# RWKV preparation in a decoder layer: which engine issues the stores of the planes and the bonus

## The chip, the cores and the metric

The kernel runs on one core of a Trainium2 chip. A core has five engines, each with a queue of instructions of its own that it works off strictly in order: TensorE (PE) multiplies matrices, VectorE (DVE) and ScalarE (ACT) work element by element, GpSimd (POOL) does a few side jobs, and SyncE (SP) does no arithmetic and only issues DMAs. A DMA can be issued from ACT's queue as well as from SP's. The engines wait for one another through semaphores, and an instruction that waits holds up everything behind it in its own queue, DMA issues included.

The metric is the device time of the whole program in microseconds (us), the median of three runs. One more run was recorded by the hardware profiler; rows of its trace are quoted below. All times in a trace are counted from the start of its span.

## What is computed

One layer of a decoder, in float32, on 1024 tokens of width 1024: a SwiGLU half-step, then three mixers side by side (RWKV-7, sliding-window attention, cross-attention into 256 memory tokens) with a gate for each, then a second SwiGLU half-step. The change lies in the RWKV mixer. Cut to what matters there:

```python
def rwkv7_mix(p, mu, w0, w_up, a0, a_up, g_up, k_k, k_a, r_k, gn_g, gn_b):
    p = p + (p_prev - p) * mu
    r, k, v, wd, ad, gd = _split(p, RWKV_SIZES)
    w_log = -jax.nn.softplus(-(w0 + jnp.tanh(wd) @ w_up)) - 0.5
    decay = jnp.exp(-jnp.exp(w_log))
    a = jax.nn.sigmoid(a0 + ad @ a_up)
    kk = (k * k_k).reshape(B, S, H, N)
    kk = kk / jnp.maximum(jnp.sqrt(jnp.sum(kk * kk, axis=-1, keepdims=True)), 1e-12)
    k = k * (1.0 + (a - 1.0) * k_a)
    y = rwkv7_recurrence(r, decay, k, v, -kk, kk * a)
    ...
    y = y + jnp.sum(r * k * r_k, axis=-1, keepdims=True) * v
```

Here `p` is the projection of the normed tokens by `w_in`. The kernel runs the recurrence in chunks of 64 tokens: a preparation makes, for every pair of heads, five arrays per token ("planes": two that hold b and k with their decays, called `bk`, then `at`, `r` and `v`) and the last line's term (the "bonus", `m`), and stores them in DRAM. A later stage inverts a small triangular matrix per chunk, and a chain over the 16 chunks reads the planes back.

## The kernel before

**Tiles and stages.** Everything is held with features on the 128 partitions and tokens along the free axis, in halves of 512 tokens. In order of time: memory keys, first SwiGLU, the RWKV preparation (`rwkv_prep`, about 740 to 920 us of the trace), eight blocks of attention projections and eight of gates on TensorE while VectorE inverts (`rwkv_invert`), the chain (`rwkv_chain`), attention with the rest of the gates, the output projection, and the second SwiGLU.

**Weights.** A float32 product is made of three matmuls (`mm3`, L330 to L332): high part by high part, high by low, low by high. Each piece of weights of 128x512 is loaded by SP into one of five buffers `w_raw` (L255), ScalarE rounds it into `w_hi` (L264), VectorE subtracts to get `w_lo` (L266). There are eight pairs of `w_hi` and `w_lo`, so a cast at L264 waits until TensorE has done with the pair from eight pieces ago, and a load at L255 waits until L266 has read its buffer.

**The preparation.** `rwkv_prep` runs over four pairs of heads, numbered 0 to 3. For each it calls `rwkv_block` for k, r and v. A block is 48 matmuls of 128x512 into two PSUM banks `pr`, and two copies by ScalarE (L820) from there into `raw`; four banks serve these blocks, so a block can start once the block two before it has been copied out. Small products stand between the blocks' matmuls: `lora` (L891, decays of the next pair), `ss` (L850, sums of squares of k), `ab` (L963, the small matrices that are inverted) and `rk` (L850, the sums in the bonus). From a copied k block come, in turn, `k` (DVE L822, L823), its square (ACT L927, shown as `n`), the parts `ss_hi` (ACT L410) and `n_lo` (DVE L411), and then the `ss` products. The decays give `sz` (ACT L893, DVE L895 and the running sum L896) and `ep` (ACT L901).

**Stores.** The small matrices `ab` go out by SP (L967), from a single buffer. The five planes (L973, 512 KB each, in pieces of 256 bytes) and the bonus (L974, 512 KB in pieces of 4 KB) go out by ScalarE in `bonus()`, once per pair: 24 stores.

**What sets the order.** The kernel is written in a tile framework: a scheduler decides, when the program is built, in which place each instruction stands in its engine's queue, from its own estimate of when inputs will be ready, from priorities, and from a few orders that the code fixes (`keep_in_program_order`). So the text of the code doesn't give the order in a queue, and moving one kind of instruction to another queue can shift others.

Of the kernel before, what the change touches and what calls it, by code (L numbers as in the profile page):

```python
# [53 lines left out]
C = 64  # L54
# [153 lines left out]
class Builder:  # L208
# [650 lines left out]
    def rwkv_prep(self, u, pool, pk_d, ab_d, bonus_d, att_d):  # L859
        nc = self.nc  # L860
        V, S = nc.vector, nc.scalar
        keep = self.tc.keep_in_program_order
        t4 = lambda n: pool.tile([P, T], F32, tag="t4", name=n)
        ch = lambda x: x.rearrange("p (c t) -> p c t", t=C)
        smask = pool.tile([P, T], mybir.dt.bfloat16, name="smask", bufs=1)
        nc.gpsimd.memset(smask, 1.0)
        nc.gpsimd.memset(ch(smask)[:, :, 0:1], 0.0)
        low = t4("low")
        self.rwkv_block(12, u, low)
        S.activation(low[0:64], low[0:64], ACT.Tanh)  # L870
        low_hi, low_lo = self.raw_part("rawl", "low_hi"), pool.tile([P, T], F32R, name="low_lo", bufs=1)
        self.split(low, low_hi, low_lo)
        gd = t4("gd")
        self.rwkv_block(13, u, gd)
        S.activation(self.sg, gd, ACT.Tanh, scale=0.5)
        V.tensor_scalar(self.sg, self.sg, 1.0, None, ALU.add)
        heads = [(slice(q * 64, q * 64 + 64), q) for q in (0, 1)]
        plane = lambda n: pool.tile([P, NC_, C], F32, tag="plane", name=n, bufs=8)
        t4r = lambda n: pool.tile([P, T], F32R, tag="t4", name=n)

        def decays(p):
            sz, a = t4("sz"), t4("a")
            w = self.lora[:, p * P : (p + 1) * P]
            w_hi, w_lo = (pool.tile([P, P], F32R, name="lora_" + t, bufs=1) for t in ("hi", "lo"))
            self.split(w, w_hi, w_lo)
            for h in (0, 1):
                cols = slice(h * TH, (h + 1) * TH)
                to = [(sz, slice(0, 64), self.half_w0, self.psum("lora")), (a, slice(64, 128), self.half_a0, self.psum("lora"))]
                for i, (w, x) in enumerate(((w_hi, low_hi), (w_hi, low_lo), (w_lo, low_hi))):
                    for _, rows, _, ps in to:  # L890
                        keep(nc.tensor.matmul(ps, w[rows], x[rows, cols], start=i == 0, stop=i == 2))  # L891
                for dst, _, bias, ps in to:
                    S.activation(dst[:, cols], ps, ACT.Tanh, scale=0.5, bias=bias[:, p : p + 1])  # L893

            V.tensor_scalar(sz, sz, 1.0, None, ALU.add)  # L895
            V.tensor_tensor_scan(sz, smask, sz, 0.0, ALU.mult, ALU.add)  # L896
            ep = t4("ep")

            tables = keep(S.preload_act_table_set("natural_log_exp_and_others"))
            with self.tc.issue_after(tables.ins):  # L900
                S.activation(ep, sz, ACT.Exp, scale=-0.5 * DECAY)  # L901
                S.activation(sz, sz, ACT.Exp, scale=0.5 * DECAY)
            S.copy(self.wc[:, :, p], ch(ep)[:, :, C - 1])
            return sz, a, ep

        later = {"k": {}, "r": {}}
        for p in range(NPAIR):
            if p == 0:
                v = plane("v")

                self.rwkv_block(8 + p, u, v)
                k = t4("k")
                self.rwkv_block(4 + p, u, k)
                made = [decays(p)]
            elif p == 1:
                k = t4("k")
                self.rwkv_block(4 + p, u, k, {**later["k"], 2: lambda: made.append(decays(p))})
            else:
                k = t4("k")
                self.rwkv_block(4 + p, u, k, later["k"])  # L920
            em, a, ep = made.pop()

            at = plane("at")
            V.scalar_tensor_tensor(at[:, :, 1:], ch(k)[:, :, 1:], self.neg_kk[:, p : p + 1], ch(ep)[:, :, : C - 1], ALU.mult, ALU.mult)
            S.activation(at[:, :, 0], ch(k)[:, :, 0], ACT.Copy, scale=self.neg_kk[:, p : p + 1])
            n2 = t4("n2")
            S.activation(n2, k, ACT.Square, scale=self.vec("rwkv_k_k", p))  # L927
            n2_parts = self.halves_split("ss", n2, t4r("n2_lo"))
            m = t4("m")
            S.activation(m, a, ACT.Identity, scale=self.half_ka[:, p : p + 1], bias=self.one_ka[:, p : p + 1])  # L930
            V.scalar_tensor_tensor(a, a, 1.0, em, ALU.add, ALU.mult)
            V.tensor_tensor(m, m, k, ALU.mult)
            bk = [plane("bk") for _ in heads]
            for rows, q in heads:
                V.tensor_tensor(bk[1 - q][rows], ch(m)[rows], ch(em)[rows], ALU.mult)

            def normed():
                for h, cols, ps in self.head_sums(*n2_parts):
                    V.tensor_scalar(n2[:, cols], ps, 1e-24, None, ALU.max)
                S.activation(n2, n2, ACT.Ln)  # L940
                S.activation(n2, n2, ACT.Exp, scale=-1.0, bias=self.ln_half)

            r = plane("r")
            self.rwkv_block(p, u, r, {**later["r"], 7: normed})
            V.scalar_tensor_tensor(ch(m), ch(m), self.vec("rwkv_r_k", p), r, ALU.mult, ALU.mult)
            V.tensor_tensor(r, r, ch(ep), ALU.mult)
            V.tensor_tensor(a, a, n2, ALU.mult)
            for rows, q in heads:
                V.scalar_tensor_tensor(bk[q][rows], ch(k)[rows], self.vec("rwkv_k_k", p)[rows], ch(a)[rows], ALU.mult, ALU.mult)
            m_parts = self.halves_split("rk", m, t4r("m_lo"))  # L950

            if p:
                v = plane("v")

            def gram(p=p, at=at, bk=bk):

                for half in (0, 1):
                    ps = self.psum("ab")
                    for c in range(8):

                        for rows, q in heads[::-1]:
                            cc = half * 8 + c
                            keep(nc.tensor.matmul(ps[rows, c * C : (c + 1) * C], bk[q][rows, cc], at[rows, cc], start=True, stop=True))  # L963
                    ab = pool.tile([P, 8, C], F32, tag="ab", name="ab", bufs=1)
                    V.tensor_tensor(ab, ps.rearrange("p (c t) -> p c t", t=C), self.gmask[:, 0:1, :].broadcast_to([P, 8, C]), ALU.mult)
                    for q in (0, 1):
                        nc.sync.dma_start(ab_d[half * 8 : (half + 1) * 8, p, q].rearrange("c s t -> s c t"), ab[q * 64 : q * 64 + 64])  # L967

            def bonus(p=p, parts=m_parts, m=m, planes=(*bk, at, r, v)):
                for h, cols, ps in self.head_sums(*parts):  # L970
                    V.tensor_tensor(ch(m[:, cols]), ch(ps), planes[4][:, h * 8 : (h + 1) * 8, :], ALU.mult)
                for i, x in enumerate(planes):
                    nc.scalar.dma_start(pk_d[:, :, p, i * C : (i + 1) * C].rearrange("c p t -> p c t"), x)  # L973
                nc.scalar.dma_start(bonus_d[p], m)  # L974

            if p == 0:

                later = {"k": {6: gram}, "r": {2: bonus}}
            else:
                within = {3: lambda: made.append(decays(p + 1))} if p + 1 < NPAIR else {}  # L980
                self.rwkv_block(8 + p, u, v, {**within, 7: gram})
                later = {"k": {5: bonus}, "r": {}}

        for i, f in enumerate(ATT_BLOCKS[:ATT_FIRST]):
            self.att_block(f, u, att_d, lambda: t4("att"), later["k"] if i == ATT_FIRST - 1 else {})
# [705 lines left out]
```

## Time and profile before

| | |
|---|---|
| median of three runs | 2321.53 us (2320.19 to 2323.29) |
| the profiled execution, its own time | 2316.22 us |
| its span, first to last instruction | 2314.5 us |
| mean granted TensorE clock | 0.994 |
| TensorE busy | 98% of the span |
| VectorE, ScalarE, GpSimd busy | 72%, 44%, 4% |
| DMA | 417.68 MB, 180 GB/s on average |

TensorE is busy nearly all the time. So what counts in a stage is the little time in which TensorE is idle, and the clock it is granted while it runs. A row of a timeline gives the start and the length of an instruction in us, the engine and the line, what it writes and reads, and in brackets how long its engine had been idle and what ended that. "ACTq" and "SPq" mark the issue of a DMA from that engine's queue.

### The profile page before, as it was taken

Reading aid. Unit: us, or ns where it says so; the run is one execution under the profiler, and the core shown is the slowest. Engines: PE = TensorE matmul, PEld = TensorE weight load, DVE = VectorE, ACT = ScalarE, POOL = GpSimd, SP = SyncE. Lnnn points to the kernel's source line nnn. Section 1 sums busy time; section 2 is a strip of 40 time slices with the busy share of each in tenths; the row PEclk is TensorE's granted clock in tenths of the full one; section 3 lists DMA queues with packets and bytes.
Section 4 is the critical chain, followed back from the end, with each engine's and each line's share of the span. In section 5 each row is a group of like instructions: output and inputs, shape, how many; then the busy total and the mean of one; then the engine's idle time right before and its main releaser. Section 6 shows DMA issues by size and latency. Waiting matters only on the chain. (4 is left out here: it accounts for less than half of the span.)

```text
span 2314.5 us, 33492 instructions
## 1 busy us (share of the span) xinstructions
PE 2263.2 (98%) x11914; PEld 1847.6 (80%) x11914; DVE 1656.0 (72%) x2683; ACT 1008.1 (44%) x1856; POOL 94.9 (4%) x134
## 2 busy tenths in 40 slices
PE   8999999999999999999999999999989999999997
PEld 6778888888888777888878877878868778888887
DVE  6998666665698786995645466575899886666576
ACT  6522333454566553223444454235762223345452
POOL 0000000000000000001300000340000000000000
PEclk9999999999999999999999999999999999999999
DMA  7477544586644447325445334554456774557663
GB/s 271 166 264 249 178 150 168 170 293 201 192 164 156 108 119 193 121 96 180 142 139 176 122 108 151 189 176 168 167 188 233 260 249 167 169 189 268 207 192 118
DMA packets 280776, 417.68 MB, mean 180 GB/s; under 512 B 82304, under 2 KB 104320, under 8 KB 280352
## 3 DMA queue, kind: packets, MB, share of 16 engines
q1 hardware_dynamic: 231552, 388.20, 50.6%
q10 hardware_dynamic: 49056, 27.34, 4.3%
q8 instruction: 94, 1.54, 0.3%
q14 instruction: 74, 0.61, 0.1%
HBM read 284.89 MB, written 129.50 MB: 179 GB/s over the span
## 5 line engine op out<-in xcount | busy, mean ns | idle before, releaser
L264 ACT CAST w_hi<-w_raw 128x512 fp32r<-128x512 f32 x594 | 365.5, 619 | 732.7 <-PE px L331 138.4
L266 DVE TENSOR_TENSOR w_lo<-w_raw,w_hi 128x512 fp32r<-128x512 f32 x594 | 413.6, 699 | 219.3 <-ACT w_hi L264 196.1
L331 PE MATMUL po<-u,w_hi 128*128 128x512 f32 (+1 forms) x476 | 181.0, 380 | 0.0
L330 PE MATMUL po<-u,w_hi 128*128 128x512 f32 (+1 forms) x476 | 181.0, 380 | 0.0
L332 PE MATMUL po<-u,w_lo 128*128 128x512 f32 (+1 forms) x476 | 181.0, 380 | 0.0
L330 PE MATMUL pgate<-u,w_hi 128*128 128x512 f32 x384 | 155.5, 405 | 0.0
L332 PE MATMUL pgate<-u,w_lo 128*128 128x512 f32 x384 | 151.3, 394 | 0.0
L330 PE MATMUL px<-f,w_hi 128*128 128x512 f32 x352 | 139.6, 397 | 11.4 <-DVE u L604 8.6
L331 PE MATMUL pgate<-u,w_hi 128*128 128x512 f32 x384 | 149.8, 390 | 0.0
L330 PE MATMUL px<-u,w_hi 128*128 128x512 f32 x352 | 137.5, 391 | 4.5 <-ACT w_hi L264 2.3
L331 PE MATMUL px<-f,w_hi 128*128 128x512 f32 x352 | 138.2, 393 | 0.3 <-DVE f L411 0.2
L332 PE MATMUL px<-f,w_lo 128*128 128x512 f32 x352 | 137.9, 392 | 0.0
L331 PE MATMUL px<-u,w_hi 128*128 128x512 f32 x352 | 137.0, 390 | 0.8 <-DVE u L411 0.8
L330 PE MATMUL pz<-u,w_hi 128*128 128x512 f32 x352 | 137.1, 390 | 0.2 <-DVE m L604 0.2
L331 PE MATMUL pz<-u,w_hi 128*128 128x512 f32 x352 | 137.2, 390 | 0.0
L332 PE MATMUL px<-u,w_lo 128*128 128x512 f32 x352 | 137.0, 389 | 0.0
L332 PE MATMUL pz<-u,w_lo 128*128 128x512 f32 x352 | 137.0, 389 | 0.0
L411 DVE TENSOR_TENSOR u<-hid,u 128x512 fp32r<-128x512 f32 x114 | 78.3, 689 | 45.2 <-ACT u L410 44.4
L331 PEld LDWEIGHTS po<-u,w_hi 128*128 128x128 f32 x476 | 89.5, 188 | 17.1
L330 PEld LDWEIGHTS po<-u,w_hi 128*128 128x128 f32 x476 | 89.5, 188 | 17.1
L332 PEld LDWEIGHTS po<-u,w_lo 128*128 128x128 f32 x476 | 89.5, 188 | 16.9
L410 ACT CAST u<-hid 128x512 fp32r<-128x512 f32 x114 | 70.7, 620 | 64.9 <-DMA hid<-form_d 56.5
(357 smaller groups left out, 5149.7 us busy)
## 6 DMA issues: line engine op xcount, KB each, us to landing
w_raw<-in_ffn_in SPq DMA_DIRECT2D x220, 256.0 KB
hid<-form_d SPq DMA_DIRECT2D x154, 256.0 KB
w_raw<-in_win SPq DMA_DIRECT2D x112, 256.0 KB
ws<-in_ffn_out SPq DMA_DIRECT2D x88, 256.0 KB
form_d<-g SPq DMA_DIRECT2D x88, 256.0 KB
ffn_sum_d<-ws SPq DMA_DIRECT2D x88, 256.0 KB
w_raw<-ffn_sum_d SPq DMA_DIRECT2D x88, 256.0 KB
form_d<-h SPq DMA_DIRECT2D x66, 256.0 KB
```

What stands on the lines that cost most here:

```text
L264: self.nc.scalar.copy(hi, x)
L266: self.nc.vector.tensor_tensor(lo, x, hi.bitcast(F32), ALU.subtract)
L330: mm(out, wh, xh, start=first, stop=False, **kw)
L331: mm(out, wh, xl, start=False, stop=False, **kw)
L332: mm(out, wl, xh, start=False, stop=last, **kw)
L410: self.nc.scalar.copy(hi, x)
L411: self.nc.vector.tensor_tensor(lo, x, hi.bitcast(F32), ALU.subtract)
```

## The change

The 24 stores of the planes and the bonus are issued from SP's queue instead of ScalarE's. Their sources, their destinations and their sizes stay as they are.

```diff
                 for i, x in enumerate(planes):
-                    nc.scalar.dma_start(pk_d[:, :, p, i * C : (i + 1) * C].rearrange("c p t -> p c t"), x)
-                nc.scalar.dma_start(bonus_d[p], m)
+                    nc.sync.dma_start(pk_d[:, :, p, i * C : (i + 1) * C].rearrange("c p t -> p c t"), x)
+                nc.sync.dma_start(bonus_d[p], m)
```

In the built program the scheduler then also places other instructions differently, in the preparation and in the inversion behind it. Three places matter in what follows.

The first is ScalarE's queue while pair 1 is finished and pair 2 begun (`raw<-pr` is here the copy of the k block of pair 2). Before:

```order
L899 ACT_TABLE_LOAD
L973 DMA pk_d<-bk 128x16x64
L901 ACTIVATE ep<-sz 128x1024
L973 DMA pk_d<-r 128x16x64
L264 COPY w_hi<-w_raw 128x512
L902 ACTIVATE sz<-sz 128x1024
L903 COPY wc<-ep 128x16
L973 DMA pk_d<-v 128x16x64
L974 DMA bonus_d<-m 128x1024
L820 COPY raw<-pr 128x512 x2
```

In the changed program, at the same place:

```order
L899 ACT_TABLE_LOAD
L901 ACTIVATE ep<-sz 128x1024
L264 COPY w_hi<-w_raw 128x512
L902 ACTIVATE sz<-sz 128x1024
L903 COPY wc<-ep 128x16
L820 COPY raw<-pr 128x512
L264 COPY w_hi<-w_raw 128x512
L820 COPY raw<-pr 128x512
```

The four stores are gone, and the cast at L264 ahead of L902 is now one that waits for a matmul in the middle of the k block itself; before, it waited for the second last matmul of the r block, which comes a whole block later. The two copies now stand around the cast that waits for the end of the k block.

The second place is VectorE's queue in pair 1, from the mask of the first `ab` of pair 0 to the low part of the square of k. Before:

```order
L895 TENSOR_SCALAR sz<-sz 128x1024
L965 TENSOR_TENSOR ab<-ab,gmask 128x512
L896 TENSOR_SCALAR sz<-smask,sz 128x1024
L971 TENSOR_TENSOR m<-rk,v 128x512 x2
L822 TENSOR_TENSOR k<-raw 128x1024
L266 TENSOR_TENSOR w_lo<-w_raw,w_hi 128x512
L965 TENSOR_TENSOR ab<-ab,gmask 128x512
L823 TENSOR_SCALAR k<-k,vecs,raw 128x1024
```

In the changed program:

```order
L965 TENSOR_TENSOR ab<-ab,gmask 128x512
L895 TENSOR_SCALAR sz<-sz 128x1024
L896 TENSOR_SCALAR sz<-smask,sz 128x1024
L822 TENSOR_TENSOR k<-raw 128x1024
L971 TENSOR_TENSOR m<-rk,v 128x512
L823 TENSOR_SCALAR k<-k,vecs,raw 128x1024
L266 TENSOR_TENSOR w_lo<-w_raw,w_hi 128x512
L965 TENSOR_TENSOR ab<-ab,gmask 128x512
L924 TENSOR_SCALAR at<-k,neg_kk,ep 128x16x63
L411 TENSOR_TENSOR n_lo<-n_7257,ss_hi 128x512 x2
```

What moved is small on VectorE; on TensorE the four `ss` products of each pair moved with it. Before, they stood 15, 48, 36 and 36 matmuls behind the end of the r block of pairs 0 to 3; now they stand directly behind it in all four.

The third place is SP's queue in pairs 0 and 1, with the loads of weights at L255. Before:

```order
L255 DMA w_raw<-in_win 128x512 x14
L967 DMA ab_d<-ab 64x8x64 x2
L255 DMA w_raw<-in_win 128x512
L967 DMA ab_d<-ab 64x8x64 x2
L255 DMA w_raw<-in_win 128x512 x5
```

In the changed program, a piece from pair 1:

```order
L255 DMA w_raw<-in_win 128x512
L973 DMA pk_d<-at 128x16x64
L255 DMA w_raw<-in_win 128x512
L973 DMA pk_d<-r 128x16x64
L973 DMA pk_d<-bk 128x16x64
L255 DMA w_raw<-in_win 128x512
L973 DMA pk_d<-bk 128x16x64
L967 DMA ab_d<-ab 64x8x64
```

The stores now stand between the loads of weights and the stores of `ab`.

## Prediction

> **What bounds the kernel now.** I read the page first, for the busy shares.
>
> ```profile
> span 2314.5 us, 33492 instructions
> PE 2263.2 (98%) x11914; PEld 1847.6 (80%) x11914; DVE 1656.0 (72%) x2683; ACT 1008.1 (44%) x1856; POOL 94.9 (4%) x134
> ```
>
> TensorE is the bound: a change gains only what TensorE stands still or runs at a lowered clock, and loses only what makes it stand still longer. The stores lie between 740 and 920 us, so next come windows there (busy time of each engine, granted clock PEclk, DMA share, GB/s).
>
> ```profile
> 740.00:920.00 180.00, 174.29 (x978) 138.36 (x977) 139.24 (x152) 89.47 (x134) 3.74 (x14) 0.99 0.53 132
> 830.80:834.20 3.40, 0.00 (x0) 0.00 (x0) 0.69 (x1) 2.10 (x5) 0.00 (x0) 1.00 1.04 200
> 835.70:839.10 3.40, 3.40 (x9) 2.65 (x8) 2.84 (x3) 1.36 (x2) 0.00 (x0) 0.50 0.30 121
> 875.70:878.00 2.30, 0.14 (x2) 0.07 (x1) 0.69 (x1) 1.32 (x4) 0.00 (x0) 1.00 0.73 143
> ```
>
> Of 180 us TensorE is busy 174.29, so 5.7 us are all that it is idle in the preparation, and nearly all of it lies in the second and the fourth stretch. The third runs at half the clock. The waits of 740 to 930 us (sum, count, longest) name what it waits for.
>
> ```profile
> PE pr L330 <- ACT raw L820: 5.6, 2, 3.4
> ACT w_hi L264 <- PE pr L331: 47.7, 20, 4.4
> ACT w_hi L264 <- DMA w_raw<-in_win: 2.1, 1, 2.1
> SPq L255 <- DVE w_lo L266: 142.7, 34, 10.4
> ```
>
> Twice, 5.6 us in all, the v block's first matmul waits for the copy of the k block (L820) out of the PSUM banks. ScalarE otherwise waits for TensorE, and for a load of weights only once. SP waits 142.7 us for buffers: its queue is mostly empty. The timeline shows the first stall (pair 2) and the second (pair 3).
>
> ```profile
> 827.68 0.39 PE L332 MATMUL pr<-u,w_lo 128*128 128x512 f32 x1
> 830.40 0.39 PE L332 MATMUL pr<-u,w_lo 128*128 128x512 f32 x1
> 830.60 0.62 ACT L264 CAST w_hi<-w_raw 128x512 fp32r<-128x512 f32 x1 [2.29 <-PE pr L331]
> 830.61 0.37 ACTq L973 DMA_DIRECT2D pk_d<-v  x1
> 831.07 2.47 ACTq L974 DMA_DIRECT2D bonus_d<-m  x1
> 831.13 1.05 ACT L902 ACTIVATE sz<-sz 128x1024 f32<-128x1024 f32 x1
> 833.59 1.07 ACT L820 COPY raw<-pr 128x512 f32<-128x512 f32 x2 [1.30 <-issue]
> 834.22 0.50 PE L330 MATMUL pr<-u,w_hi 128*128 128x512 f32 x1 [3.43 <-ACT raw L820]
> ...
> 875.58 0.62 ACT L264 CAST w_hi<-w_raw 128x512 fp32r<-128x512 f32 x1 [2.76 <-PE pr L331]
> 876.05 1.20 ACTq L974 DMA_DIRECT2D bonus_d<-m  x1
> 877.30 1.07 ACT L820 COPY raw<-pr 128x512 f32<-128x512 f32 x2 [0.97 <-issue]
> 877.94 0.50 PE L330 MATMUL pr<-u,w_hi 128*128 128x512 f32 x1 [2.16 <-ACT raw L820]
> ```
>
> At 830.40 the last matmul of the r block of pair 2 starts. The banks of the k block, finished a whole block earlier, are still not copied, because in ScalarE's queue the copy stands behind a cast that waits for the end of the r block (2.29 us idle until 830.60), then L902, and then the issue of the bonus store, 2.47 us, of which 1.30 keep ScalarE idle. Pair 3 shows the same with 0.97 us of issue. So each stall has two causes in one queue: the place of the copy, and the price of the issue ahead of it. From 827.68 to 830.40 lie twelve steps, which makes 0.227 us for one matmul at full clock.
>
> **The change part by part.** *The stalls.* In the changed order the copy of the k block in pairs 2 and 3 stands at the k block's own end, around the cast for that end, and no store is ahead of it. The v block then finds its banks free a block (48 × 0.227 = 10.9 us) early: −3.43 and −2.16 us. *The clock.* The stretch at half clock begins 1.5 us after the first stall ends. Nine matmuls take 3.40 us where fifteen fit (1.4 us lost), and 0.50 of 3.40 us is 1.7; I take 1.6. No such stretch follows the stall of 2.16 us, so a stall between 2.2 and 3.4 us is what brings it on here. With the stall gone: −1.6 us.
>
> The Trainium skill, "TensorE: Matmul & The Clock Gate", section "Part 1: The HAM clock gate", says that the clock drops to half after at least one idle window of about 3.4 us, and that the windows run free of the program. The two stalls of the trace agree with it, and by it 3.43 us only just trips the gate, so timed runs of the kernel before may have been without the stretch.
>
> *The new place of `ss`.* The four `ss` products of each pair now stand directly behind the r block. They were 15 to 48 matmuls later, so what makes `n_lo` has lost up to 10.9 us of cover. Its pieces, by form (count | busy us, mean ns | idle before):
>
> ```profile
> L896 DVE TENSOR_TENSOR_SCAN sz<-smask,sz 128x1024 f32<-128x1024 bf16 x4 | 9.1, 2286 | 0.1
> L901 ACT ACTIVATE ep<-sz 128x1024 f32<-128x1024 f32 x4 | 4.2, 1059 | 2.7 <-DVE sz L896 2.7
> L895 DVE TENSOR_SCALAR sz<-sz 128x1024 f32<-128x1024 f32 x4 | 2.8, 689 | 3.5 <-ACT sz L893 3.5
> L820 ACT COPY raw<-pr 128x512 f32<-128x512 f32 x20 | 10.6, 580 | 2.3 <-issue 2.3
> L822 DVE TENSOR_TENSOR k<-raw 128x1024 f32<-128x1024 f32 x4 | 4.9, 1221 | 4.4 <-ACT raw L820 4.4
> L971 DVE TENSOR_TENSOR m<-rk,v 128x512 f32<-128x512 f32 x8 | 5.1, 673 | 0.0
> L823 DVE SCALAR_TENSOR_TENSOR k<-k,vecs,raw 128x1024 f32<-128x1024 f32 x4 | 5.1, 1281 | 0.1
> L266 DVE TENSOR_TENSOR w_lo<-w_raw,w_hi 128x512 fp32r<-128x512 f32 x35 | 24.0, 688 | 33.2 <-ACT w_hi L264 32.6 <-PE ss L850 0.4
> L965 DVE TENSOR_TENSOR ab<-ab,gmask 128x512 f32<-128x512 f32 x8 | 5.5, 686 | 1.8 <-DMA ab_d<-ab 1.6 <-DMA w_raw<-in_win 0.2
> L924 DVE SCALAR_TENSOR_TENSOR at<-k,neg_kk,ep 128x1008 f32<-128x1008 f32 x4 | 5.1, 1269 | 1.4 <-ACT ep L901 1.2
> L893 ACT ACTIVATE a<-lora,half_a 128x512 f32<-128x512 f32 x8 | 5.5, 686 | 0.0
> L411 DVE TENSOR_TENSOR n_lo<-n,ss_hi 128x512 fp32r<-128x512 f32 x8 | 5.1, 685 | 1.4 <-ACT ss_hi L410 1.4
> 903.57 2.08 PE L963 MATMUL ab<-at,bk 64*64 64x64 f32 x64
> ```
>
> Pair 1 is the tight one, because there the second copy stands behind `ep`. From the end t of the k block: a cast (0.6, as at 830.60), two of L893 (1.37), L895 (0.69) and the scan L896 (2.29) make t + 5.0; `ep` 1.06 and the copy 0.58 make 6.6; on VectorE L822, L971, L823, L266, L965 and L924 (5.82) make 12.4, and both `n_lo` (1.37) 13.8. TensorE arrives after the r block (10.9), a batch of `ab` (2.08) and four `rk` (0.9): t + 13.9. Margin zero; hand-overs between the engines can make it 1.3 us late, as long as the two `n_lo`. In pair 0 the same products come within a few tenths of their inputs; in pairs 2 and 3 both copies stand at the block's end, which takes some 6 us off this chain. I take +0.5 us for all, of 0 to 1.5.
>
> *The stores on SP.* Their issue costs what it costs on ScalarE, 0.37 (830.61) to 2.47 us (831.07) each: 24 of them 9 to 59 us, against 142.7 us in which SP waits for buffers. They can also hold SP until their source is written; the nearest rows are the stores of `ab` on the same queue.
>
> ```profile
> SPq L967 <- DVE ab L965: 10.6, 6, 3.5
> q10 hardware_dynamic: 41856, 12.58, 31.6%
> q1 hardware_dynamic: 13286, 10.92, 20.9%
> ```
>
> That is 1.8 us for each wait, for 24 stores 42 us; even with the dearest issue, 101 of 142.7 us. Queue q10 holds what ScalarE issued, 12.58 MB (24 × 0.52) in 31.6% of 180 us = 56.9 us, that is 2.4 us a store over the 16 engines. Together with q1's 37.6 us the ring of SP would carry 94.5 of 180 us. With five buffers and 34 loads (the waits of L255 above) in 180 us, a load has four casts' time, some 21 us, less its own flight, before its cast wants it; the six stores of a pair in a row are 14 us. So nothing from the side of the loads: 0, where the other end is the third rival below.
>
> *Behind the preparation.* The same matmuls follow. The inversion reads `ab` once its last store has landed, so its end moves with the preparation's, and its result is early anyway:
>
> ```profile
> 1058.86 1.92 SPq L1021 DMA_DIRECT2D dinv<-inv_d  x2
> 1071.86 0.51 PE L1013 MATMUL z<-z,dinv 64*64 64x64 f32 x10
> ```
>
> The issue is 13 us before the first use, so a few us of delay there would cost nothing.
>
> **Sum:** −3.43 − 2.16 − 1.6 + 0.5 = −6.7 us. Against the profiled execution's own 2316.22 (span 2314.5 and 1.7 around it) that is 2309.5. The median of the three runs is 5.3 above that execution, by something that no trace shows, so I carry the difference over: 2321.53 − 6.7 = **2314.8 us**.
>
> **Rivals.** *Only the issue goes.* The copies might still come late (if the order at run time is set by another wait), and what is saved is the idle of the issue, 1.30 + 0.97 = 2.3 us: 2319.2; with the first stall then at 2.1 us and the half clock gone too, 2317.6. For it: the rows at 833.59 and 877.30 say "issue". Against it: the wait of 2.29 us ahead of the cast at 830.60 stands before the copy and has no part in the issue.
>
> The Trainium skill, "DMA: Bandwidth & Descriptors", section "Issuing engines are not separate DMA queues", speaks for this one: DMAs of all engines run over the same 16 DMA engines, and issuing from another engine saves only that sequencer's time to initiate, usually little. By it the change is worth the 2.3 us at most. Here the row at 831.07 shows 2.47 us for one issue, and an in-order queue behind it.
>
> *The `ss` products become the wait.* VectorE's second mask of `ab` (L965) may only write once the earlier store of `ab` has landed, and that store now stands on the same queue behind loads and planes. L965 above waited 1.6 us for it in all, with the planes on another queue; one plane of 2.4 us ahead, in pairs 1 to 3, makes three stalls of about 2.4 us: 7.2 lost for 7.2 gained, 2321.5. Two planes ahead make 4.8 us each, over the length that brought on the half clock: 3 × (4.8 + 1.6) − 7.2 = +12, 2333.5. Against it: six us of slack in pairs 2 and 3.
>
> *Loads held behind the stores (slower).* A store on SP whose source isn't written yet stops all loads behind it. The place is SP's queue between L255 and L973; it decides once a load is later than the 21 us less its flight. Then casts (L264) wait for DMA, and since the copies L820 stand behind casts, each pair could have a stall like the one at 834.22: 4 × (3.43 + 1.6) − 7.2 = +12.9, 2334.4. For it: single waits of SP for a buffer reach 10.4 us already, and the planes are made late in a pair. Against it: the sums above, 101 of 142.7 and 94.5 of 180.
>
> *The half clock isn't there in the timed runs.* Then 1.6 us less is gained: 2316.4, still faster.
>
> **How the numbers follow.** About 0.2% (4.6 us) is what a measurement of this kernel can tell from no change: faster is below 2316.9, slower above 2326.2. The forecast, with or without the half clock, gets 0.55 (0.53 faster, 0.02 same); only the issue 0.13 (same); the `ss` wait 0.15 (0.05 faster, as a small one; 0.07 same; 0.03 slower); loads held 0.12 (slower); something not seen 0.05 (0.01, 0.02, 0.02). Faster 0.59, same 0.24, slower 0.17. The likeliest case alone spans 2312 (nothing new waits and the timed runs lose more to the clock) to 2317. The range takes in the issue case and the `ss` wait: 2311 to 2324.
>
> **What would show it.** Right: in 740 to 920 us TensorE busy for all but a few tenths, the granted clock 1.00, no wait of L330 for L820; copies of k in pairs 2 and 3 within a us of the k block's end; at most 1.3 us of waiting of `ss` for L411 in pair 1; L264 waiting for TensorE and not for `w_raw`; SP's wait for L266 smaller but still tens of us; the inversion's load some 7 us earlier. Wrong: `ss` products waiting over 1.5 us, casts waiting for loads, a new stretch at 0.50, or a gain in the preparation that the chain gives back by waiting for `dinv`.

## The result, and the profile after

| | before | after |
|---|---|---|
| median | 2320.43 us (8 runs, 2317.05 to 2323.29) | 2313.24 us (8 runs, 2306.71 to 2317.63) |
| after to before | | 0.9973, 95% interval 0.9964 to 0.9983 |
| the profiled execution, its own time | 2316.22 us | 2312.79 us |

The change makes the kernel 7.2 us faster by the medians; 2314.8 us was predicted. The two profiled executions lie only 3.4 us apart. To see what the change itself does, one measures the stretch that holds all that it moves: from the first `lora` product (L891) to the first product of the chain (L1013), with the same matmuls in between. Their views by line (shortest, median and longest ns, first and last start) of the kernel before:

```profile
L891 PE MATMUL lora<-low_hi,lora_hi x16: 389/496/502, 749.7 to 850.8; 64*128 64x512 f32 x16
...
L1013 PE MATMUL y<-center,f x256: 217/218/267, 1067.5 to 1165.0; 64*64 64x64 f32 x128
```

And of the kernel after:

```profile
L891 PE MATMUL lora<-low_hi,lora_hi x16: 388/495/500, 750.8 to 839.5; 64*128 64x512 f32 x16
...
L1013 PE MATMUL y<-center,f x256: 218/218/267, 1062.1 to 1159.4; 64*64 64x64 f32 x128
```

With the starts to the hundredth, the stretch has 317.75 us before and 311.26 after: 6.49 us less. It is called "the stretch" below. The first rows show why whole times are a blunt measure here: the kernel after came 1.1 us later to its preparation. Windows of the first SwiGLU, which the change doesn't touch, show a part of it; the first is the kernel after, the second the kernel before:

```profile
151.30:154.60 3.30, 3.30 (x9) 2.57 (x10) 2.72 (x5) 0.00 (x0) 0.00 (x0) 0.51 0.61 181
```

```profile
151.30:154.60 3.30, 3.30 (x15) 2.56 (x15) 3.18 (x6) 0.23 (x1) 0.00 (x0) 1.00 0.78 274
```

This execution of the kernel after had a spell at half clock there (0.51), the one of before had none. The same kernel, run once more (e8 below), has none at this place: such spells come and go between executions of one kernel.

The window of the preparation in the kernel after:

```profile
740.00:920.00 180.00, 176.71 (x1007) 143.04 (x1006) 140.26 (x153) 90.59 (x138) 2.89 (x14) 1.00 0.58 146
```

TensorE is busy 176.71 us there instead of 174.29, at a granted clock of 1.00 instead of 0.99. No matmul waits for a copy. By form, the matmuls of 740 to 930 us of the kernel after that still wait (count | busy us, mean ns | idle before them):

```profile
L963 PE MATMUL ab<-at,bk 64*64 64x64 f32 x256 | 8.3, 219 | 2.3 <-ACT w_hi L264 1.6 <-ACT a L893 0.4 <-DVE bk L949 0.3
L891 PE MATMUL lora<-low_hi,lora_hi 64*128 64x512 f32 x16 | 4.2, 456 | 0.4 <-DVE n L939 0.3
...
L850 PE MATMUL ss<-n_lo,bones_r 128*128 128x512 f32 x8 | 3.3, 407 | 0.7 <-DVE n_lo L411 0.7
```

The idle of 5.6 us before L330 is gone; 3.4 us of idle before small products are new. The timeline of ScalarE shows the copies of the k block of pair 2, which answer to the row at 833.59 of before:

```profile
820.88 0.59 ACT L820 COPY raw<-pr 128x512 f32<-128x512 f32 x1 [0.56 <-PE pr L332]
821.36 0.62 ACT L264 CAST w_hi<-w_raw 128x512 fp32r<-128x512 f32 x1
821.88 0.59 ACT L820 COPY raw<-pr 128x512 f32<-128x512 f32 x1
```

They now wait for the block itself (0.56 us for its last matmul). The two largest new waits, in pairs 1 and 2, in the timeline of the kernel after:

```profile
792.13 1.29 DVE L411 TENSOR_TENSOR n_lo<-n,ss_hi 128x512 fp32r<-128x512 f32 x2
793.47 0.50 PE L850 MATMUL ss<-n_lo,bones_r 128*128 128x512 f32 x1 [0.66 <-DVE n_lo L411]
...
846.56 1.28 DVE L949 SCALAR_TENSOR_TENSOR bk<-k,vecs,a 64x1024 f32<-64x1024 f32 x1
847.35 0.61 ACT L264 CAST w_hi<-w_raw 128x512 fp32r<-128x512 f32 x1
847.99 0.41 PE L963 MATMUL ab<-at,bk 64*64 64x64 f32 x7 [1.55 <-ACT w_hi L264]
```

The last row names ScalarE's cast, since that ended last before the start, but the products read `bk`, and VectorE finishes `bk` at 846.56 + 1.28 = 847.84. Why VectorE is so late there is taken up below. SP's waits in 740 to 930 us, where the stores now are:

```profile
SPq L255 <- DVE w_lo L266: 93.0, 30, 7.1
SPq L973 <- DVE bk L949: 16.3, 6, 8.3
SPq L973 <- DVE at L924: 11.8, 3, 7.6
```

SP holds a store up to 8.3 us until its source is written, and still waits 93 us for buffers of weights.

### The profile page after: what moved, and what is told of

The parts are those of the page before. It is cut to its first block, busy times and chain, and to the rows that moved or that the text cites. A ratio compares the mean times of both kernels' runs of the same rounds, so it can differ in the third digit from the quotient of the medians.

```text
span 2311.1 us, 33503 instructions
## 1 busy us (share of the span) xinstructions
PE 2260.1 (98%) x11914; PEld 1846.5 (80%) x11914; DVE 1657.2 (72%) x2683; ACT 1007.7 (44%) x1856; POOL 94.6 (4%) x134
## 5 line engine op out<-in xcount | busy, mean ns | idle before, releaser
L264 ACT CAST w_hi<-w_raw 128x512 fp32r<-128x512 f32 x594 | 365.3, 619 | 693.3 <-PE px L331 147.0
L330 PE MATMUL po<-u,w_hi 128*128 128x512 f32 (+1 forms) x476 | 180.9, 380 | 0.0
L330 PE MATMUL pgate<-u,w_hi 128*128 128x512 f32 x384 | 155.4, 405 | 0.0
L330 PE MATMUL px<-f,w_hi 128*128 128x512 f32 x352 | 140.5, 400 | 13.4 <-DVE u L604 10.1
L330 PE MATMUL px<-u,w_hi 128*128 128x512 f32 x352 | 137.4, 390 | 3.4 <-ACT vm L1296 1.4
L330 PE MATMUL pz<-u,w_hi 128*128 128x512 f32 x352 | 137.0, 390 | 0.2 <-DVE m L604 0.2
L330 PEld LDWEIGHTS po<-u,w_hi 128*128 128x128 f32 x476 | 89.5, 188 | 16.9
```

The lines of the kernel that those rows point to most:

```text
L264: self.nc.scalar.copy(hi, x)
L330: mm(out, wh, xh, start=first, stop=False, **kw)
```

## The experiments

All ratios are to the kernel before, run again on the same chip in the same set; medians of different sets can't be compared (that of the kernel before lies between 2319.97 and 2322.24 us in them). The stretch comes from each kernel's one trace.

| kernel | median, us | ratio, 95% interval | stretch, us | against before |
|---|---|---|---|---|
| before | 2320.43 | | 317.75 | |
| the change | 2313.24 | 0.9964 to 0.9983 | 311.26 | −6.49 |
| e1, only the bonus on SP | 2320.17 | 0.9981 to 1.0000 | 317.91 | +0.17 |
| e2, only the planes on SP | 2316.88 | 0.9964 to 0.9988 | 312.22 | −5.53 |
| e3, stores as before, copies first | 2323.15 | 0.9989 to 1.0008 | 317.01 | −0.74 |
| e4, the change, `ab` later | 2313.69 | 0.9945 to 0.9975 | 310.19 | −7.55 |
| e5, stores as before, copies and `ss_hi` first | 2308.59 | 0.9935 to 0.9962 | 308.89 | −8.85 |
| e6, the change, every store twice | 2334.60 | 1.0055 to 1.0081 | 335.77 | +18.02 |
| e7, the change, fewer waits | 2308.05 | 0.9936 to 0.9961 | 308.30 | −9.45 |
| e8, the change again | 2310.06 | 0.9944 to 0.9970 | 310.99 | −6.76 |
| e9, the change, `lora` split | 2312.17 | 0.9953 to 0.9977 | 310.54 | −7.21 |
| e10, as e7, `ab` later still | 2310.18 | 0.9939 to 0.9966 | 308.33 | −9.41 |
| e11, as e10, the last `ab` later too | 2310.87 | 0.9938 to 0.9963 | 307.87 | −9.87 |
| e12, as e11, stores on ScalarE | 2309.07 | 0.9933 to 0.9957 | 307.66 | −10.09 |

e8 is the yardstick: 

> The changed kernel itself once more, as a yardstick: the preparation 6.5 us shorter than before within 0.5 us, with the same four new waits of ss, ab and lora; the whole program differs from the first profile by up to 3 us through stretches at half clock in other stages.

It gave −6.76: this one repeat of the changed kernel lies within 0.3 us. The kernel before was traced only once.

### e1 and e2: one kind of store alone

e1 moves only the last line's store, e2 only the planes':

```diff
-                nc.scalar.dma_start(bonus_d[p], m)
+                nc.sync.dma_start(bonus_d[p], m)
```

> Only the four bonus stores move to SP; the twenty plane stores stay on ScalarE, and the order on TensorE stays that of before. Theory (the place of the copy in ScalarE's queue is the larger cause): the k copies still stand behind the cast for the r block's end, so L330 waits for L820 about 3.43 - 1.30 = 2.1 us and 2.16 - 0.97 = 1.2 us, 3.3 us in all instead of 5.6; the half clock behind the first stall is gone (1.6 us); the preparation gains 2.3 to 3.9 us. Rival (the price of the issue is the cause): both stalls vanish and it gains as much as the whole change, 6 to 7 us.

> Only the twenty plane stores move to SP; the four bonus stores, whose issues of 2.47 and 1.20 us stood ahead of the late copies, stay on ScalarE. The order on TensorE is that of the changed kernel. Theory (order): no wait of L330 for L820, the same new waits of the ab and ss products (about 3 us in all), gain in the preparation 6 to 7 us as with the whole change. Rival (issue): the issues of the bonus still hold the copies, L330 waits for them about 2 us in pairs 2 and 3 and the gain falls to 2 to 4 us.

TensorE's timeline of e1, at the two old stalls and one new one:

```profile
805.49 0.47 PE L850 MATMUL ss<-n_lo,bones_r 128*128 128x512 f32 x1 [2.50 <-DVE n_lo L411]
...
837.98 0.50 PE L330 MATMUL pr<-u,w_hi 128*128 128x512 f32 x1 [2.03 <-ACT raw L820]
...
879.03 0.50 PE L330 MATMUL pr<-u,w_hi 128*128 128x512 f32 x1 [1.08 <-ACT raw L820]
```

The stalls fell from 3.43 to 2.03 and from 2.16 to 1.08 us: by 1.40 and 1.08, which is what the issue rows of before promised (1.30 and 0.97). The rest of each stall stays, as the theory had it. But the expected gain was not kept: `ss` of pair 1 waits 2.50 us. ScalarE's timeline of e1 shows why:

```profile
798.23 1.14 ACT L927 ACTIVATE n<-k,vecs 128x1024 f32<-128x1024 f32 x1
...
802.79 0.62 ACT L264 CAST w_hi<-w_raw 128x512 fp32r<-128x512 f32 x1 [3.43 <-PE pr L331]
803.32 1.14 ACT L410 CAST ss_hi<-n 128x512 fp32r<-128x512 f32 x2
```

`n` is ready at 799.4, but the scheduler now put a cast that waits for the end of the v block of pair 1 ahead of `ss_hi`. In the kernel before, `ss_hi` stood ahead of that cast. So the same trap opened at another place, by the shift of one store. A stretch at half clock followed this stall (the last section shows it). In e2 no wait of L330 for a copy is left although the issues of the bonus stay on ScalarE, and the stretch is 5.53 us shorter: 1.0 to 1.2 us short of the whole change. Some 0.7 us of that are longer waits in pair 2 (`ab` 1.91 us instead of 1.55, and 0.35 of `ss`), and there VectorE had waited 3.81 us instead of 2.67 for a store of `ab` to land. What is left isn't shown to be a cost of the four issues.

### e3 and e5: no store moved

e3 gives only the copies a higher priority:

```diff
-                nc.scalar.copy(raw[:, 8 + h * TH : 8 + (h + 1) * TH], ps[h])
+                with self.tc.high_priority(offset=30):
+                    nc.scalar.copy(raw[:, 8 + h * TH : 8 + (h + 1) * TH], ps[h])
```

> All 24 stores stay on ScalarE; only the copies at L820 get a higher priority, which puts the copies of the k block at that block's end in pairs 2 and 3. Theory (order): the two stalls and the half clock go without any store moved: 5.6 + 1.6 = 7.2 us less in the preparation, with the lora products still in three groups per pair, and the ss products late as before, so without the new waits of ss; up to 1 us may come back elsewhere. Rival (issue): the stores' issues delay ScalarE wherever the copies stand, and TensorE waits 2 us or more for copies, casts or ss_hi; gain under 4 us.

The stalls at L330 went, and the gain failed to come. TensorE's timeline of e3 (its lines are one higher than before's):

```profile
849.17 0.50 PE L851 MATMUL ss<-n_lo,bones_r 128*128 128x512 f32 x1 [2.41 <-DVE n_lo L411]
...
891.52 0.47 PE L851 MATMUL ss<-n_lo,bones_r 128*128 128x512 f32 x1 [2.50 <-DVE n_lo L411]
```

and the rows of ScalarE in front of the first of them:

```profile
846.57 0.62 ACT L264 CAST w_hi<-w_raw 128x512 fp32r<-128x512 f32 x1 [2.41 <-PE pr L331]
846.81 0.37 ACTq L974 DMA_DIRECT2D pk_d<-at  x1
847.09 1.14 ACT L410 CAST ss_hi<-n 128x512 fp32r<-128x512 f32 x2
```

Neither theory had this: the copies came out of the trap and `ss_hi` fell into it, in pairs 2 and 3. `ss_hi` follows the cast at once, with no idle time for the issue that stands between them, which speaks against the stores' issue as the cause. The stall lasts as long as the work behind the released cast: 2.60 us from its start to `ss` here, 2.69 in pair 3 (from 888.83), 2.70 in e1 (from 802.79). That the cast itself waited 2.41 us, like TensorE, is a coincidence; in e1 it waited 3.43 for a stall of 2.50. Half clock followed the stall of 2.50 in pair 3 and took its part of the gain too. e5 tests the order: it adds the same priority for the square of k and its parts.

```diff
-            S.activation(n2, k, ACT.Square, scale=self.vec("rwkv_k_k", p))
-            n2_parts = self.halves_split("ss", n2, t4r("n2_lo"))
+            with self.tc.high_priority(offset=30):
+                S.activation(n2, k, ACT.Square, scale=self.vec("rwkv_k_k", p))
+                n2_parts = self.halves_split("ss", n2, t4r("n2_lo"))
```

> All 24 stores stay on ScalarE, as before; the copies (L820) and the square of k with its parts (Square, ss_hi, n_lo) get a higher priority, so that in ScalarE's queue neither stands behind a cast that waits for a later matmul. On TensorE the lora products stand in six groups instead of ten. Theory (order alone): no wait of L330 for the copies and none of ss for n_lo; the preparation loses 7.5 us of stalls and half clock, and some 0.4 us for each of the four lora groups that are gone, 1.6 us: 8 to 9.5 us less than before, more than the change itself with its 6.5. Rival (the stores' issue on ScalarE costs by itself, wherever the other instructions stand): TensorE waits 2 us or more for ScalarE's late products and the gain stays under 6 us.

All 24 stores are still on ScalarE, and the stretch is 8.85 us shorter, more than the change brings. By form, in e5:

```profile
L330 PE MATMUL pr<-u,w_hi 128*128 128x512 f32 x179 | 70.3, 393 | 0.0
...
L851 PE MATMUL ss<-n_lo,bones_r 128*128 128x512 f32 x8 | 3.3, 407 | 0.0
```

Neither waits any more. The order alone does it, without a store moved. Some 2 us of the 8.85 are fewer breaks at the `lora` products (see e9): steps of 0.31 to 0.35 us went from 41 to 29, and three of the four of about 0.43 us are gone. The rest are stalls and the half clock.

### e4, e7, e10 and e11: the change's own waits

e4 emits `ab` of pairs 1 and 2 a little later:

```diff
-                self.rwkv_block(8 + p, u, v, {**within, 7: gram})
-                later = {"k": {5: bonus}, "r": {}}
+                self.rwkv_block(8 + p, u, v, {**within, 7: gram} if p + 1 == NPAIR else within)
+                later = {"k": {5: bonus} if p + 1 == NPAIR else {0: gram, 5: bonus}, "r": {}}
```

> The changed kernel with the ab products of pairs 1 and 2 emitted at the start of the next k block instead of at the end of the v block; on TensorE this puts pair 2's ab four matmuls (0.9 us) later. Theory (the changed kernel's own new wait, 1.55 us of ab for VectorE's bk in pair 2, comes from ab standing too early): that wait falls by 0.9 us to 0.7 us, the rest stays: 0.9 us less than the changed kernel. Rival (what makes bk is itself late by the wait of VectorE, so that whatever comes next waits): no gain, the wait only moves to another product.

In TensorE's timeline of e4 the wait of 1.55 us has become

```profile
848.24 0.47 PE L963 MATMUL ab<-at,bk 64*64 64x64 f32 x9 [0.57 <-ACT w_hi L264]
```

0.98 us less for four matmuls (0.9 us), and nothing waits in its place: −7.55 against −6.49. e7 goes on with that. It adds e3's priority for the copies, and the `ab` of pair 0 and the decays of pair 1 come later:

```diff
-                self.rwkv_block(4 + p, u, k, {**later["k"], 2: lambda: made.append(decays(p))})
+                self.rwkv_block(4 + p, u, k, {**later["k"], 4: lambda: made.append(decays(p))})
...
-                later = {"k": {6: gram}, "r": {2: bonus}}
+                later = {"k": {}, "r": {0: gram, 2: bonus}}
...
-                later = {"k": {5: bonus} if p + 1 == NPAIR else {0: gram, 5: bonus}, "r": {}}
+                later = {"k": {5: bonus} if p + 1 == NPAIR else {2: gram, 5: bonus}, "r": {}}
```

> The changed kernel (stores on SP) with the copies at a higher priority, ab of pair 0 two and of pairs 1 and 2 four to sixteen matmuls later, and the decays of pair 1 two pieces later. It aims at the changed kernel's own waits: lora for n 0.8, ab 0.5 + 1.7 + 0.5, ss 0.8, together 4.3 us. Theory (all of them are products placed ahead of what VectorE can deliver): 3 to 4 us less than the changed kernel in the preparation, that is 9.5 to 10.5 us less than before. Rival (VectorE is the bound there, the waits move to what comes next): less than 1 us gained on the changed kernel.

−9.45, just short of the 9.5 to 10.5 that were expected; 1.00 us of idle before `ab` of pair 0 and some 0.4 in pair 3 stay. e10 and e11 push those away too (`{1: gram, 3: bonus}` in pair 0 and `{3: gram, 6: bonus}` in pairs 1 and 2; e11 also `{0: gram, 5: bonus}` in pair 3):

> The kernel e7_fewer_waits with ab of pairs 0, 1 and 2 six more matmuls later. Theory (ab stands ahead of what VectorE delivers): of its two waits left, 1.17 us (pair 0) falls to 0 and 0.56 us (pair 3, not moved) stays; preparation 10.5 us less than before. Rival (VectorE is behind by then and the wait goes to rk, which comes next): no less than 9.5.

> As e10, with ab of pair 3 twenty-three matmuls (5 us) later too; the small matrices go out some 5 us later and the inversion begins that much later. Theory (the inverse is early by 12 us or more, as the prediction had it): preparation 11 us less than before, and the chain gives nothing back. Rival (the chain waits for dinv): a new wait of the chain, up to 5 us given back.

e10 missed: −9.41 instead of −10.5. The wait of pair 0 went, but 0.49 us came back as a wait of `ss` for `n_lo` in pair 1 (not at `rk`, where the rival had it), and three more long steps at changes of shape (25 instead of 22; see e9) came with the new order. e11 brought 0.46 us more, about the wait of pair 3 that it removes, and its chain gives nothing back though the last `ab` starts 4.2 us later (887.65 instead of 883.48).

### e12: the same with the stores on ScalarE

e12 is e11 with the 24 stores back on ScalarE's queue and the square of k at e5's priority.

> As e11, with all 24 stores on ScalarE as before and the square of k at a higher priority, so that the order is free of the late copies and late ss_hi; lora in four groups. Theory (the queue of the stores matters only through the order): preparation within 1.5 us of e11. Rival (24 issues on ScalarE cost by themselves): waits of TensorE for ScalarE's products of 3 us or more that e11 doesn't have.

307.66 against 307.87 us of stretch, and medians whose intervals overlap: once the order is good, the queue of the stores makes no difference that can be measured. The two orders aren't the same one: the priority of the square also shifts small products in e12. No run has the changed kernel's own order with all stores on ScalarE.

### e6: twice the stores

The changed kernel, in which all six stores of `bonus()` are issued a second time from SP.

> The changed kernel with every plane and bonus stored twice from SP, 48 stores instead of 24; pair 2's ab stands ten matmuls later than in the changed kernel. Theory (SP and its DMA ring have room): the casts at L264 don't wait for loads; the preparation is within 1 us of the changed kernel's, or up to 1.7 us shorter where pair 2's ab no longer waits. Rival (loads are held behind stores, and the changed kernel is close to that edge): casts wait for w_raw, TensorE loses 3 us or more in the preparation.

The time came out as the rival had it, 0.7% slower, but at another place than it named. The casts don't wait for loads. TensorE's one long wait in e6, with the copy it waits for:

```profile
946.90 1.07 ACT L1344 COPY att<-pq 128x512 f32<-128x512 f32 x2 [14.95 <-DMA att_d<-att]
947.54 0.80 PE L330 MATMUL pq<-u,w_hi 128*128 128x512 f32 x1 [16.01 <-ACT att L1344]
```

It is the attention copies behind the preparation that need a buffer whose store, also on SP, is stuck behind the planes of the last pair. A spell at half clock begins within the stall and lasts 3.4 us beyond it, and the chain waits 3.0 us for the load of the planes (`f`), which adds to the loss. So SP and its ring do have an edge, between 24 and 48 stores, and it is met where several stores of one pair come in a row.

### e9: the grouping of `lora`

The twelve `lora` products of pairs 2 and 3 are issued in three groups of four, at pieces 3, 4 and 5 of the v block:

```diff
-                within = {3: lambda: made.append(decays(p + 1))} if p + 1 < NPAIR else {}
+                d = decays(p + 1) if p + 1 < NPAIR else None
+                within = {3: lambda: next(d), 4: lambda: next(d), 5: lambda: made.append(next(d))} if d else {}
```

with `decays` made a generator that pauses after each of its three kinds of product.

> The changed kernel with the twelve lora products of pairs 2 and 3 issued in three groups of four, with six matmuls of the v block between them, instead of in one group: four groups more in the preparation. Theory (each change between the 64-row lora products and the 128-row matmuls costs TensorE about 0.1 us at four places, 0.4 us for a group): 1.7 us more at such changes than in the changed kernel, about eight to sixteen more steps of 0.31 to 0.35 us instead of 0.227. Rival (the grouping costs nothing, the difference between before and after had another source): as many such steps as in the changed kernel, 23, and no loss outside the waits that the trace names.

TensorE's timeline of e9 around one such group:

```profile
839.17 0.39 PE L331 MATMUL pr<-u,w_hi 128*128 128x512 f32 x1
839.40 0.39 PE L332 MATMUL pr<-u,w_lo 128*128 128x512 f32 x1
839.72 0.73 PE L892 MATMUL lora<-low_hi,lora_hi 64*128 64x512 f32 x4
840.38 0.50 PE L330 MATMUL pr<-u,w_hi 128*128 128x512 f32 x1
840.72 0.40 PE L331 MATMUL pr<-u,w_hi 128*128 128x512 f32 x1
```

From one 128-row matmul to the next is 0.23 us; into the group it is 0.32, and the matmul behind the group takes 0.34 until the next starts. In the stretch, steps of 0.31 to 0.35 us went from 23 to 40, 1.7 us in all, as expected. The stretch still is 0.7 us shorter than the changed kernel's, because the split also moved `ss` and `ab` and 2.6 us of their waits went (0.4 came back at `lora`); without the count of steps the two effects would have been taken for one.

## Why the prediction came out right

**The stalls and the half clock** (−3.43, −2.16 and −1.6): right, and for the reason given. All three are gone from the trace. e1 shows that each stall had two causes, as the prediction split them (issue 1.30 and 0.97; with the bonus issues gone the stalls are 1.40 and 1.08 shorter), and that with the issue alone removed the stalls keep 2.03 and 1.08 us.

**New waits** (+0.5, of 0 to 1.5): too small. They are 3.4 us, where the prediction's sign for being right was idle time of a few tenths. Of these `ss` of pair 1 is 0.66, within the bounds that the chain of pair 1 gave (margin zero, up to 1.3 late). What the prediction left out is `ab`: it followed the `ss` products to their new place but not the products behind them. Counted in TensorE's order, `ab` of pair 2 stood 108 matmuls behind the end of its r block and stands 50 behind it after the change, and VectorE's chain to `bk` isn't done by then: 1.55 us. e4 shows this price directly.

That chain began late, by a wait that the prediction had named in its second rival. VectorE's second mask of `ab` of pair 1, just ahead of the `k` of pair 2, waits for an earlier store of `ab` to land. Its rows in the kernel after, on SP's queue and on VectorE's:

```profile
815.41 0.74 SPq L967 DMA_DIRECT2D ab_d<-ab  x1
820.00 0.34 SPq L255 DMA_DIRECT2D w_raw<-in_win  x1
820.40 0.59 SPq L967 DMA_DIRECT2D ab_d<-ab  x1
```

```profile
823.84 0.69 DVE L965 TENSOR_TENSOR ab<-ab,gmask 128x512 f32<-128x512 f32 x1 [2.67 <-DMA ab_d<-ab]
```

The second store of that half stands behind a load of weights that is issued only at 820.00. From the start of `k` (825.05) to the end of `bk` (847.84) VectorE is idle only 1.1 us, so the delay reaches `bk`. e8, the same program, shows how nearly whole it arrives; there the two waits are

```profile
819.90 0.69 DVE L965 TENSOR_TENSOR ab<-ab,gmask 128x512 f32<-128x512 f32 x1 [2.39 <-DMA ab_d<-ab]
844.05 1.15 PE L963 MATMUL ab<-at,bk 64*64 64x64 f32 x32 [1.27 <-ACT w_hi L264]
```

Both are shorter by 0.28 us. So the place of `ab` on TensorE and the place of its stores on SP make this wait together; no run moves those stores alone.

**A gain that the prediction didn't have**: about 2.6 us. Ahead of the change, `lora` of pairs 1 to 3 came in three groups each with matmuls of another shape between them; after it, in one. In the kernel before, a single `lora` product cost this:

```profile
805.30 0.40 PE L330 MATMUL pr<-u,w_hi 128*128 128x512 f32 x1
805.53 0.39 PE L331 MATMUL pr<-u,w_hi 128*128 128x512 f32 x1
805.85 0.50 PE L891 MATMUL lora<-low_hi,lora_hi 64*128 64x512 f32 x1
806.28 0.50 PE L332 MATMUL pr<-u,w_lo 128*128 128x512 f32 x1
806.62 0.40 PE L330 MATMUL pr<-u,w_hi 128*128 128x512 f32 x1
```

Steps of 0.32, 0.43 and 0.34 us where 0.23 is usual. Ten such groups became four: 18 fewer steps of 0.31 to 0.35 (1.8 us) and four of about 0.43 (0.8 us). So the sum is −7.2 + 3.4 − 2.6 = −6.4 against −6.49 measured. The predicted −6.7 is close because two terms that were wrong, +2.9 and −2.6, nearly cancel. That is luck: the number is less well founded than it looks.

**Stores on SP at no cost, nothing lost behind the preparation**: right for the loads. SP's waits for buffers fell from 142.7 to 93.0 us, no cast waits for a load, the inversion's load starts at 912.9 instead of 920.39, and in the chain its products (L1013) wait 1.0 us for VectorE, after as before. In e6 the cover does run out, but at twice the stores. The landing of `ab` above is a cost on SP's queue that this term doesn't have; the prediction left it to the second rival.

**The rivals.** "Only the issue goes" is what e1 does to the two stalls, not what the change does. "The `ss` products become the wait" holds for 0.66 us in pair 1, through the chain of k. Its mechanism, the landing of `ab`, is there in pair 2 (2.67 us of VectorE), where `ss` has the slack that the prediction saw; it comes out at the next product, `ab`, which the rival didn't price. "Loads held behind the stores" isn't there with 24 stores.

**What the prediction took for the cause.** It saw that the copies' place in the order was one part of the stalls, but it didn't ask whether a good order needs the stores moved at all. The runs say that it doesn't: e5 and e12, with all stores on ScalarE, gain more, and e1 and e3, which move one store kind or only the copies, gain nothing. The long stalls of before, e1 and e3 all stand behind a cast that waits for a later matmul of TensorE and is, in ScalarE's queue, ahead of something that TensorE needs sooner. The changed kernel's own waits have another source: VectorE's chains, and in pair 2 the landing of `ab` behind loads on SP.

## What to carry to other kernels

Where an engine works for two customers in one in-order queue, look for the instruction in it that waits for TensorE, and ask what behind it TensorE waits for; the stall is as long as the work that still follows once that instruction is released. Where a scheduler sets the order, price an edit by every small product that it shifts, those behind the first one too, and try the order itself (a priority) before moving work to another queue. Products of another shape belong together: each group of them that is broken up costs TensorE time at both ends.

## What the hardware showed

**A change of shape costs TensorE time.** Between products with 64 rows (`lora`) and matmuls with 128, steps are about 0.1 us longer at some four places for each group (0.32, 0.33 and 0.34 instead of 0.227 us), 1.7 us for four groups more in e9. The Trainium skill, "TensorEngine Tiling (Array Packing)", section "Key Properties", says that a change of the tiling mode drains TensorE; the longer steps agree with it and give the change this price here, though no row shows a drain itself.

**The half clock doesn't go by the length of one stall.** The prediction took it that a stall between 2.2 and 3.4 us is what brings it on. In e1 the stall of 2.50 us at 805.49 was followed by this window:

```profile
806.50:809.90 3.40, 3.40 (x11) 2.27 (x11) 3.39 (x5) 0.06 (x1) 0.10 (x1) 0.50 0.01 2
```

The stall of 2.50 us of e3 at 891.52 was followed by one too; that of 2.41 in e3 at 849.17 was not, nor that of 2.03 in e1. These alone would fit a limit between 2.41 and 2.50 us. But in the first SwiGLU a single stall of 1.95 us (e5, at 151.45) was followed by half clock, and one of 2.38 us (e7, at 150.54) was not:

```profile
152.80:156.00 3.20, 3.20 (x9) 2.54 (x8) 2.08 (x4) 0.00 (x0) 0.00 (x0) 0.50 0.73 230
```

```profile
150.60:154.00 3.40, 3.40 (x15) 2.70 (x16) 3.40 (x6) 0.41 (x1) 0.00 (x0) 1.00 0.88 268
```

So no limit on the length of one stall sorts them, and the prediction's reading holds only for the two stalls that it was taken from. The Trainium skill, "TensorE: Matmul & The Clock Gate", section "Part 1: The HAM clock gate", asks for at least one idle window of about 3.4 us; stalls of 1.95 and 2.50 us were enough here, and the measurement decides. That the windows run free of the program, as the same section of the Trainium skill says, would fit stalls of nearly one length with and without it; no run here shows the windows themselves.
